# Attention scores of a hybrid encoder: two products over 128 rows, or three over 64 rows with two heads side by side

## The chip, the core and the metric

The kernel runs on one core of a Trainium2 chip. The engines of the core that matter here are TensorE (PE; its weight loads are shown as PEld), VectorE (DVE), ScalarE (ACT), GpSimd (POOL) and SyncE (SP), whose queue issues nearly all DMAs. The metric is device time in microseconds, lower is better: before the change the median of three runs was 1366.57 us (1365.75 to 1369.16).

## The reference

Two layers of an encoder over 512 tokens of width 1024, in fp32. Each layer adds to x a mixer of two head groups, a cross attention to 256 memory tokens, and a gated feed-forward block with a convolution of width 3. The change touches the scores of the mixer alone:

```python
def hybrid_mixer(h, w_in, rpb, q_norm, k_norm, w_out, rows, cos, sin):
    proj = h @ w_in
    na_q, na_k, na_v, g_q, g_k, g_v = jnp.split(proj, IN_SPLIT_POINTS, axis=-1)
    na_out = neighbourhood_attention(na_q, na_k, na_v, rpb, rows)      # 8 heads of 64
    g_q = apply_axial_rope(rms_norm(g_q, q_norm), cos, sin)            # 8 heads of 64
    g_k = apply_axial_rope(rms_norm(g_k, k_norm), cos, sin)            # 2 heads of 64
    gqa_out = gqa_block_attention(g_q, g_k, g_v)
    return jnp.concatenate([na_out, gqa_out], axis=-1) @ w_out

# neighbourhood_attention
scores = jnp.einsum('brqhd,brikhd->bhrqik', q, k_rows) * (dh ** -0.5)
# gqa_block_attention, one block of 128 queries
sc = jnp.einsum('bqkgd,bskd->bkgqs', qi, k) * scale
```

A score is a sum over the 64 elements of a head. The mixer's neighbourhood attention (NA) has, for a block of 128 queries, a window of 256 keys; its grouped-query attention (GQA) looks at all 512 keys.

## The kernel before

**Arithmetic.** TensorE is given operands in a reduced fp32 form (`F32R`). To keep fp32's accuracy, each operand is held as a rounded part and the difference to it, hi and lo, and a product of two operands is made as hi*hi + hi*lo + lo*hi, three matmuls into one PSUM bank (`mm3`, L374). Values live transposed: a projection's result has 128 output channels on the partitions ("rows") and the 512 tokens on the columns, so one tile holds two heads of 64, one on rows 0 to 63, the other on rows 64 to 127.

**Scores before.** A sum over 64 elements would use half of the rows, so the kernel fills the other half with the lo part. `split_q` (L735) writes for each head j a tile with q's hi on the head's own 64 rows and its lo on the other 64. `split_k` (L717) writes for each head k's hi twice, on both halves, and k's lo twice. Two matmuls over 128 rows then give (q_hi + q_lo) * k_hi and (q_hi + q_lo) * k_lo. A result must be written to both halves, which engines do in instructions of 64 rows: each head has its own ScalarE copy (the rounding) and its own VectorE difference. The doubling of k is done by two DMAs a tile (`double`, put into SP's queue), but for the first k tile of layer 0 (`near`), where ScalarE and VectorE write both halves themselves.

**Groups.** The mixer runs in units. `na_scores` (L778) makes 8 units a layer (4 head pairs, 2 pairs of query blocks), each with 2 heads, 2 blocks, 2 products: 8 matmuls of 256 columns. `gqa_scores` (L947) makes 16 units a layer (4 head pairs, 4 query blocks), each with 2 heads, 2 products: 4 matmuls of 512 columns. Behind the scores follow a row maximum on VectorE (L797, L959), the exponential on ScalarE (L803, L961), the division (L809, L967, L522), transposes on TensorE (`na_transpose`, `gqa_transpose_p`), and the products with the values (`na_values`, `gqa_values`).

**Order.** TensorE and SP run in program order. `weave` (L170) lines the steps of several units up, each unit's steps in different rounds, and puts matmuls of other work (projections of coming heads, output projection, memory keys) between them through a `Filler`. How much filler comes in goes by a count of TensorE time, `Counted.ns` (L67), which adds for a matmul of n columns max(107, (n+32)/2.4) ns; in the GQA part each round has a slot of counted time (`GQA_SLOT`, L49), and the filler fills up what the round's own steps leave. `late(n, fn)` puts a step off by n x 3600 counted ns (the doubling DMAs by 2, the steps of the rotary embedding by 1 or 2 each). Work on ScalarE, VectorE and GpSimd is ordered by a scheduler. Projection results are read from PSUM (`split_qk` L704; tags `mm`, 4 banks, `sc`, 2 banks, `tr`, 2 banks); a bank is given to the next product when its readers are done. SBUF tiles of the tag `r` come from a pool of 21.

For the GQA heads `gqa_rope` (L895) does norm and rotation in steps: products with gain and tables on VectorE (L901, L902), a square on ScalarE (L903), a swap of rows by DMA, a sum on GpSimd, a spread of the norm on TensorE, and then `split` (L933), which calls the same `split_q` and `split_k`.

The helper that the change uses in their place exists already, for values and for the memory attention:

```python
def split_psum(hi, lo, ps, scale=None):
    if scale is None:
        read(ACT.copy(hi, ps))
        DVE.tensor_sub(lo, ps, f(hi))
```

Of the kernel before, what the change touches and what calls it, by code (L numbers as in the profile page):

```python
# [18 lines left out]
P = 128  # L19
S = 512  # L20
# [25 lines left out]


NA_FILL = 2500
GQA_SLOT = [3950] * 16 + [4200, 3300, 3000, 3000]  # L49
MEM_FILL = [1, 1, 2, 2, 1, 3, 1, 3, 1, 3, 1]  # L50
N_ROWS = 3
LATE = 3600
# [14 lines left out]
class Counted(InOrder):  # L67


    ns = 0.0  # L70

    def matmul(self, out, lhsT, rhs, **k):
        n = 1
        for d in rhs.shape[1:]:
            n *= d
        self.ns += max(107.0, (n + 32) / 2.4)
        return self.tc.keep_in_program_order(self.engine.matmul(out, lhsT, rhs, **k))  # L77


# [104 lines left out]
def encoder_kernel(ctx: ExitStack, tc: tile.TileContext, t: dict, out: bass.AP):  # L184
    nc = tc.nc
    PE, SP = Counted(tc, nc.tensor), InOrder(tc, nc.sync)
    late = Late(PE)
    ACT_IN_ORDER = InOrder(tc, nc.scalar)
    ACT, DVE, POOL = Free(nc.scalar), Free(nc.vector), Free(nc.gpsimd)
# [24 lines left out]
    def rtile(shape, dt=F32R):  # L214
        return rpool.tile([P, *shape], dt, tag="r", name=nm("r"), padded_shape=[P, *pad(shape)])
# [7 lines left out]
    def rpair():  # L223

        hl = rtile((2, S))
        return hl[:, 0, :], hl[:, 1, :]
# [13 lines left out]
    f = lambda ap: ap.bitcast(F32)  # L240
# [10 lines left out]
    def read(e):  # L251
        reads.append(e.ins)
        return e
# [362 lines left out]
    for n in FIRST:  # L616
# [10 lines left out]
        k = slice(k0, k1)  # L627
# [15 lines left out]
    for l in range(DEPTH):  # L643
# [60 lines left out]
        def split_qk(n, p, pm):  # L704
            if n == "q":
                DVE.scalar_tensor_tensor(pm, pm, HD**-0.5, mix.rep, op0=ALU.mult, op1=ALU.mult)
                st = rtile((2, S))
                qk[n, p] = [st[:, j] for j in range(2)]
                split_q(pm, st)
                return  # L710
            DVE.tensor_mul(pm, pm, mix.rep)

            kt = [rtile((2, S)) for _ in range(2)]
            qk[n, p] = [kt[j][:, part] for part in range(2) for j in range(2)]
            split_k(pm, kt, (l, p) == (0, 0))

        def split_k(pm, kt, near):  # L717
            rows = [(slice(64 * j, 64 * j + 64), slice(64 - 64 * j, 128 - 64 * j)) for j in range(2)]
            for k, (r, o) in zip(kt, rows):
                read(ACT.copy(k[r, 0], pm[r]))  # L720
                if near:
                    ACT.copy(k[o, 0], pm[r])
            for k, (r, o) in zip(kt, rows):
                DVE.tensor_sub(k[r, 1], pm[r], f(k[r, 0]))
                if near:
                    DVE.tensor_sub(k[o, 1], pm[r], f(k[r, 0]))

            def double():
                for k, (r, o) in zip(kt, rows):
                    SP.dma_start(f(k[o]), f(k[r]))  # L730

            if not near:
                late(2, double)

        def split_q(pm, st):  # L735
            halves = [(st[:, j], slice(64 * j, 64 * j + 64), slice(64 - 64 * j, 128 - 64 * j)) for j in range(2)]
            for v, r, o in halves:
                read(ACT.copy(v[r], pm[r]))  # L738
            for v, r, o in halves:
                DVE.tensor_sub(v[o], pm[r], f(v[r]))  # L740

        vblk = [None, None]

# [34 lines left out]
        def na_scores(u):  # L778
            p, bp = divmod(u, 2)
            if bp == 0 and p + 1 < 4:  # L780
                load_bias(p + 1)
            qst, kst = qk["q", p], qk["k", p]
            sc = [ps_s().rearrange("p (i n) -> p i n", i=2) for _ in range(2)]
            for i in range(2):
                b = 2 * bp + i
                qs, ks = slice(b * P, b * P + P), slice(WIN[b], WIN[b] + 256)
                for j in range(2):
                    for part in range(2):
                        PE.matmul(sc[j][:, i, :], qst[j][:, qs], kst[2 * part + j][:, ks], start=part == 0, stop=part == 1)
            nmx, sums = small(4), small(4)  # L790
            es = [tmp((2, 256)) for _ in range(2)]
            with behind(30):
                for j in range(2):
                    for i in range(2):
                        b = 2 * bp + i
                        col = slice(2 * j + i, 2 * j + i + 1)
                        DVE.tensor_tensor_reduce(  # L797
                            out=sc[j][:, i, :], in0=sc[j][:, i, :], in1=bias[p][j][:, WTYPE[b], :],
                            op0=ALU.add, op1=ALU.min, scale=-1.0, scalar=BIG, accum_out=nmx[:, col])
                for j in range(2):  # L800
                    for i in range(2):
                        col = slice(2 * j + i, 2 * j + i + 1)
                        ACT.activation(es[j][:, i, :], sc[j][:, i, :], AF.Exp, bias=nmx[:, col], scale=-1.0,  # L803
                                       accum_out=sums[:, col])
            na[u] = es, sums
# [89 lines left out]
        def gqa_rope(g, pm):  # L895


            gain = qkg[:, l, 0:1] if g != "k" else qkg[:, l, 1:2]
            xs, sq, cc = tmp(), tmp(), tmp()
            with behind(-20):  # L900
                DVE.scalar_tensor_tensor(xs, pm, gain, gtab[0][:, 1], op0=ALU.mult, op1=ALU.mult)  # L901
                DVE.scalar_tensor_tensor(cc, pm, gain, gtab[0][:, 0], op0=ALU.mult, op1=ALU.mult)  # L902
                read(ACT.activation(sq, pm, AF.Square))  # L903

            def swap():
                xr = tmp()
                for i in range(4):
                    SP.dma_start(xr[32 * i : 32 * i + 32], xs[32 * (i ^ 1) : 32 * (i ^ 1) + 32])
                pv = ps_t()
                for b in range(NB):  # L910
                    PE.matmul(pv[:, 2 * b : 2 * b + 2], sq[:, b * P : (b + 1) * P], pairs, start=True, stop=True)
                v, r = small(2 * NB), small(2 * NB)
                DVE.scalar_tensor_tensor(
                    v.rearrange("p (b j) -> p b j", j=2), pv[:, 0 : 2 * NB].rearrange("p (b j) -> p b j", j=2),
                    1.0 / HD if g == "k" else 1.0, geps[:, int(g != "k")].unsqueeze(2).to_broadcast([P, NB, 2]),
                    op0=ALU.mult, op1=ALU.add)
                rows = tmp()
                with behind(-40):
                    POOL.tensor_tensor(r, v, mhalf[:, : 2 * NB], op=ALU.pow)
                    POOL.tensor_copy(rows.rearrange("p (b d) -> p b d", d=HD), r.unsqueeze(2).to_broadcast([P, 2 * NB, HD]))  # L920
                late(1, lambda: rotate(xr, rows))

            def rotate(xr, rows):
                POOL.tensor_add(xr, cc, xr)
                late(2, lambda: norm(xr, rows))

            def norm(xr, rows):
                pr = ps_mm()
                for b in range(NB):
                    PE.matmul(pr[:, b * P : (b + 1) * P], rows[:, b * P : (b + 1) * P], ident, start=True, stop=True)  # L930
                late(1, lambda: split(xr, pr))

            def split(xr, pr):  # L933
                DVE.tensor_mul(pr, xr, pr)
                if g == "k":
                    gk.extend(rtile((2, S)) for _ in range(2))
                    split_k(pr, gk, False)
                else:
                    gq[g] = rtile((2, S))
                    split_q(pr, gq[g])  # L940

            late(1, swap)

# [3 lines left out]
        def gqa_scores(u):  # L947
            i, b = divmod(u, NB)
            qs = slice(b * P, b * P + P)
            assert gq[i] is not None and gk and gvt  # L950
            sc = [ps_s() for _ in range(2)]
            for j in range(2):
                for part in range(2):
                    PE.matmul(sc[j], gq[i][:, j, qs], gk[j][:, part], start=part == 0, stop=part == 1)
            nmx, sums = small(2), small(2)
            es = []
            for j in range(2):
                c = slice(j, j + 1)
                DVE.tensor_reduce(nmx[:, c], sc[j], axis=AX.X, op=ALU.max, negate=True)  # L959
                e = tmp()  # L960
                last_exp[0] = read(ACT.activation(e, sc[j], AF.Exp, bias=nmx[:, c], accum_out=sums[:, c])).ins  # L961
                es.append(e)
            ga[u] = es, sums
# [25 lines left out]
        def gqa_values(u, j):  # L989
# [2 lines left out]
            i, bp = divmod(u // 2, 2)  # L992
            if j == 0:
                gpo[u] = ps_mm().rearrange("p (j n) -> p j n", j=2)
            po, pts = gpo[u], gpt[u // 2]
            for k in range(NB):
                for n in range(2):
# [459 lines left out]
```

## Time and profile before

| | us |
|---|---|
| median of three runs | 1366.57 |
| profiled execution | 1367.86 |
| its span, first to last instruction | 1366.1 |
| TensorE busy in the span | 1349.0 |
| VectorE busy | 877.3 |
| ScalarE busy | 675.0 |
| GpSimd busy | 688.1 |

How to read it: in the rows of a timeline stand the start and the length in us, the engine, the line, the operation, the tiles (out<-in, with a short name for a pool's tiles), the shape and the number of instructions merged into the row; in brackets the idle time ahead of it and what ended it. The line of a matmul is that of a helper (L77 for all in-order matmuls, L64 for transposes), so products are told apart by their tiles: `sc<-r,r` are scores, `tr<-ident,t` transposes. In the groups stand the shape, the count, busy time and mean length in ns, and the idle time just before. Matmuls overlap: the length of a record is longer than the distance from one start to the next. In the rows of a window stand its limits, its length, and busy time and count of each engine (PE, PEld, DVE, ACT, POOL), then the granted TensorE clock, the DMA share and GB/s.

### The profile page before, as it was taken

How to read it: one execution, taken by the hardware profiler on the slowest of the kernel's cores; microseconds unless marked ns; L12 is line 12 of the kernel's file. 1: busy time of each engine (PE TensorE's matmuls, PEld its weight loads, DVE VectorE, ACT ScalarE, POOL GpSimd, SP SyncE). 2: the span in 40 equal slices, each digit the busy share in tenths (PEclk: the TensorE clock that was granted, in tenths of full speed). 3: DMA queues.
4: the chain of work that ended last, by engine and by line, in shares of the span. 5: the costliest groups of instructions: out<-in, count | busy, mean ns of one | idle time of the engine just before them, and what ended most of it. 6: DMA issues, size and time to landing. Idle time of an engine off the chain costs nothing.

```text
span 1366.1 us, 19239 instructions
## 1 busy us (share of the span) xinstructions
PE 1349.0 (99%) x7082; PEld 1157.5 (85%) x7082; DVE 877.3 (64%) x1542; ACT 675.0 (49%) x1258; POOL 688.1 (50%) x491
## 2 busy tenths in 40 slices
PE   9999999999999999999999999999999999999998
PEld 7888899888888888888888988998888888888897
DVE  6665776665886188357546777746758834861874
ACT  6675577564543144234456667756644423432441
POOL 2466657636444444444554676657264444444441
PEclk9999999999999999999999999999999999999999
DMA  6753213322333333333347532133143333323331
GB/s 215 212 169 99 77 47 86 86 77 77 104 98 93 95 98 92 102 94 98 87 121 227 140 101 70 57 100 94 31 123 93 101 100 93 101 84 109 93 92 63
DMA packets 219358, 139.88 MB, mean 102 GB/s; under 512 B 6144, under 2 KB 212224, under 8 KB 219264
## 3 DMA queue, kind: packets, MB, share of 16 engines
q1 hardware_dynamic: 218432, 138.13, 34.5%
q8 instruction: 56, 0.92, 0.3%
q10 hardware_dynamic: 832, 0.53, 0.1%
q14 instruction: 38, 0.31, 0.1%
HBM read 126.05 MB, written 2.10 MB: 94 GB/s over the span
## 4 chain that ended last, share of the span: by engine, by line
PE 91%; DVE 3%; ACT 3%; DMA 2%; issue 1%; SPq 0%; POOL 0%; DVEq 0%; ACTq 0%
PE mm L77 80%; PE sc L77 6%; PE tr L64 3%; PE tr L77 1%; DMA raw<-in_w_in 1%; DMA t<-in_memT 1%; ACT t L803 1%; ACT hi L290 0%; SPq L64 0%; DMA xT<-in_xT 0%; DVE t L487 0%; ACT r L515 0%; DVE sc L797 0%; DVE r L740 0%; ACT r L738 0%
## 5 line engine op out<-in xcount | busy, mean ns | idle before, releaser
L291 POOL TENSOR_TENSOR lo<-raw,hi 128x1024 fp32r<-128x1024 f32 (+2 forms) x268 | 499.9, 1876 | 477.1 <-ACT hi L290 472.7
L77 PE MATMUL mm<-xg,hi 128*128 128x512 f32 x1920 | 596.6, 392 | 0.0
L77 PEld LDWEIGHTS mm<-xg,hi 128*128 128x128 f32 x1920 | 356.7, 188 | 70.8
L290 ACT CAST hi<-raw 128x512 fp32r<-128x512 f32 (+2 forms) x276 | 224.1, 836 | 309.5 <-PE mm L77 256.3
L77 PE MATMUL mm<-xg,lo 128*128 128x512 f32 x960 | 374.5, 390 | 0.0
L77 PE MATMUL mm<-r,hi 128*128 128x512 f32 (+1 forms) x1096 | 316.6, 373 | 0.0
L77 PEld LDWEIGHTS mm<-r,hi 128*128 128x128 f32 x1096 | 198.3, 189 | 34.7 <-DVE r L516 0.4
L1281 DVE SCALAR_TENSOR_TENSOR t<-t,par,t 128x7 f32<-128x7 f32 (+1 forms) x352 | 201.8, 641 | 34.0 <-ACT t L1274 34.0
L77 PEld LDWEIGHTS mm<-xg,lo 128*128 128x128 f32 x960 | 180.7, 188 | 38.2
L77 PE MATMUL mm<-r,lo 128*128 128x512 f32 (+1 forms) x548 | 203.5, 371 | 0.0
L77 PEld LDWEIGHTS mm<-r,lo 128*128 128x128 f32 x548 | 103.3, 188 | 17.8
L1266 DVE TENSOR_TENSOR t<-mm,rep 128x512 f32<-128x512 f32 x88 | 60.1, 687 | 78.6 <-PE mm L77 62.3
L522 POOL TENSOR_SCALAR t<-t,s 128x512 f32<-128x512 f32 (+1 forms) x112 | 66.8, 610 | 78.0 <-DVE s L809 36.8
L1287 DVE TENSOR_TENSOR r<-t,r 128x512 fp32r<-128x512 f32 x44 | 90.2, 2049 | 7.3 <-ACT r L1286 4.1
L1283 ACT ACTIVATE t<-t 128x512 f32<-128x512 f32 x44 | 27.9, 633 | 134.4 <-DVE t L1281 134.3
L1310 DVE TENSOR_TENSOR xT<-xT,mm 128x512 f32<-128x512 f32 x32 | 21.9, 685 | 106.8 <-PE mm L77 106.8
L77 PE MATMUL sc<-r,r 128*128 128x256 f32 (+1 forms) x352 | 70.0, 332 | 0.0
L1274 ACT ACTIVATE t<-t,par 128x512 f32<-128x512 f32 x88 | 66.8, 806 | 3.3 <-DVE t L1266 3.3
L64 PE MATMUL tr<-ident,t 128*128 128x128 f32 x456 | 62.0, 276 | 2.3 <-DVE t L522 0.9
L77 PE MATMUL mm<-r,r 128*128 128x256 f32 (+1 forms) x428 | 61.9, 297 | 2.4 <-ACT t L903 2.4
L64 PEld LDWEIGHTS tr<-ident,t 128*128 128x128 f32 x456 | 53.3, 142 | 10.5 <-issue 2.9
L77 PEld LDWEIGHTS mm<-r,r 128*128 128x128 f32 x428 | 56.3, 191 | 5.1 <-ACT t L903 2.6
(156 smaller groups left out, 1618.2 us busy)
## 6 DMA issues: line engine op xcount, KB each, us to landing
raw<-in_w_up SPq DMA_DIRECT2D x88, 512.0 KB, 3.7
raw<-in_w_in SPq DMA_DIRECT2D x33, 512.0 KB, 3.9
raw<-in_w_down SPq DMA_DIRECT2D x32, 448.0 KB, 3.6
raw<-in_w_mem_kv SPq DMA_DIRECT2D x16, 512.0 KB, 3.6
raw<-in_w_down SPq DMA_DIRECT2D x16, 512.0 KB, 3.9
r<-in_bias SPq DMA_DIRECT2D x16, 384.0 KB, 5.6
r<-r SPq DMA_DIRECT2D x22, 256.0 KB, 5.0
raw<-in_w_out SPq DMA_DIRECT2D x8, 512.0 KB, 3.6
```

What stands on the lines that cost most here:

```text
L64: return lambda *a, **k: self.tc.keep_in_program_order(op(*a, **k))
L77: return self.tc.keep_in_program_order(self.engine.matmul(out, lhsT, rhs, **k))
L290: act.copy(hi[:, k], raw[:, k])
L291: (POOL if eng[0] == "P" else DVE).tensor_sub(lo[:, k], raw[:, k], f(hi)[:, k])
L522: eng.tensor_scalar(e, e, sums[:, col : col + 1], 1.0, op0=ALU.mult, op1=ALU.mult)
L803: ACT.activation(es[j][:, i, :], sc[j][:, i, :], AF.Exp, bias=nmx[:, col], scale=-1.0, accum_out=sums[:, col])
L1266: DVE.tensor_mul(u, us[side], ffn.rep)
L1274: ACT.activation(cc, u, AF.Identity, bias=par[:, l, CB + ch : CB + ch + 1], scale=w[1])
L1281: DVE.scalar_tensor_tensor(cc[:, dst], u[:, src], wi, cc[:, dst], op0=ALU.mult, op1=ALU.add)
L1283: ACT.activation(cs[0], cs[0], AF.Silu)
L1287: DVE.tensor_sub(acts[j][1], cs[0], f(acts[j][0]))
L1310: DVE.tensor_add(xT[m], xT[m], pm)
```

## The change

q and k are held as the projection leaves them, both heads in one tile, one tile for hi and lo: a single copy and a single difference over 128 rows. The halves are not doubled, so the DMAs and the `near` case go. A score is now three products over the 64 rows of its head, q_hi*k_hi + q_hi*k_lo + q_lo*k_hi; the two heads' products alternate, one on rows 0 to 63, the other on rows 64 to 127, each into its own bank. An NA unit has 12 matmuls in place of 8, a GQA unit 6 in place of 4. The count takes a matmul of 64 rows at half, and 150 ns for each change of the number of rows; 16 slots grow by 100 ns. The check that the value tile exists moves from the scores to the values. (lo*lo, which the two products of before included, is left out, as in `mm3`.)

```diff
-GQA_SLOT = [3950] * 16 + [4200, 3300, 3000, 3000]
+GQA_SLOT = [4050] * 16 + [4200, 3300, 3000, 3000]
...
-    ns = 0.0
+    ns, rows = 0.0, P
 
     def matmul(self, out, lhsT, rhs, **k):
...
-        self.ns += max(107.0, (n + 32) / 2.4)
+        rows = lhsT.shape[0]
+        if rows != self.rows:
+            self.ns += 150.0
+        self.rows = rows
+        self.ns += max(107.0, (n + 32) / 2.4) * rows / P
...
         def split_qk(n, p, pm):
             if n == "q":
                 DVE.scalar_tensor_tensor(pm, pm, HD**-0.5, mix.rep, op0=ALU.mult, op1=ALU.mult)
-                st = rtile((2, S))
-                qk[n, p] = [st[:, j] for j in range(2)]
-                split_q(pm, st)
-                return
-            DVE.tensor_mul(pm, pm, mix.rep)
-
-            kt = [rtile((2, S)) for _ in range(2)]
-            qk[n, p] = [kt[j][:, part] for part in range(2) for j in range(2)]
-            split_k(pm, kt, (l, p) == (0, 0))
-
-        def split_k(pm, kt, near):
...
-        def split_q(pm, st):
...
+            else:
+                DVE.tensor_mul(pm, pm, mix.rep)
+
+            qk[n, p] = rpair()
+            split_psum(*qk[n, p], pm)
+
+        def pair_scores(sc, q, k, qs, ks):
+
+            (qh, ql), (kh, kl) = q, k
+            for n, (a, b) in enumerate(((qh, kh), (qh, kl), (ql, kh))):
+                for j in range(2):
+                    r = slice(64 * j, 64 * j + 64)
+                    PE.matmul(sc[j], a[r, qs], b[r, ks], start=n == 0, stop=n == 2)
...
-                for j in range(2):
-                    for part in range(2):
-                        PE.matmul(sc[j][:, i, :], qst[j][:, qs], kst[2 * part + j][:, ks], start=part == 0, stop=part == 1)
+                pair_scores([v[:, i, :] for v in sc], qk["q", p], qk["k", p], qs, ks)
...
                 if g == "k":
-                    gk.extend(rtile((2, S)) for _ in range(2))
-                    split_k(pr, gk, False)
+                    gk.extend(rpair())
+                    split_psum(*gk, pr)
                 else:
-                    gq[g] = rtile((2, S))
-                    split_q(pr, gq[g])
+                    gq[g] = rpair()
+                    split_psum(*gq[g], pr)
...
-            assert gq[i] is not None and gk and gvt
+            assert gq[i] is not None and gk
             sc = [ps_s() for _ in range(2)]
-            for j in range(2):
-                for part in range(2):
-                    PE.matmul(sc[j], gq[i][:, j, qs], gk[j][:, part], start=part == 0, stop=part == 1)
+            pair_scores(sc, gq[i], gk, qs, slice(0, S))
...
+            assert gvt
             po, pts = gpo[u], gpt[u // 2]
```

More of the change, by code (lines that the diff above doesn't have):

```diff
@@ L706, in split_qk @@
                 DVE.scalar_tensor_tensor(pm, pm, HD**-0.5, mix.rep, op0=ALU.mult, op1=ALU.mult)
-                st = rtile((2, S))
-                qk[n, p] = [st[:, j] for j in range(2)]
-                split_q(pm, st)
-                return
-            DVE.tensor_mul(pm, pm, mix.rep)
-            kt = [rtile((2, S)) for _ in range(2)]
-            qk[n, p] = [kt[j][:, part] for part in range(2) for j in range(2)]
-            split_k(pm, kt, (l, p) == (0, 0))
-        def split_k(pm, kt, near):
[L718 to L733, printed above, removed]
-        def split_q(pm, st):
[L736 to L740, printed above, removed]
+            else:
[8 more added lines that the diff above has]
+                    PE.matmul(sc[j], a[r, qs], b[r, ks], start=n == 0, stop=n == 2)
         vblk = [None, None]
@@ L781, in na_scores @@
                 load_bias(p + 1)
-            qst, kst = qk["q", p], qk["k", p]
             sc = [ps_s().rearrange("p (i n) -> p i n", i=2) for _ in range(2)]
```

## The prediction

> **What bounds the kernel now.** I read the page first (busy shares, then the chain that ended last), then the groups by line and shape, then TensorE's own timeline around the scores, then its waits.
>
> ```profile
> span 1366.1 us, 19239 instructions
> PE 1349.0 (99%) x7082; PEld 1157.5 (85%) x7082; DVE 877.3 (64%) x1542; ACT 675.0 (49%) x1258; POOL 688.1 (50%) x491
> PE 91%; DVE 3%; ACT 3%; DMA 2%; issue 1%; SPq 0%; POOL 0%; DVEq 0%; ACTq 0%
> PE mm L77 80%; PE sc L77 6%; PE tr L64 3%; PE tr L77 1%; DMA raw<-in_w_in 1%; DMA t<-in_memT 1%; ACT t L803 1%; ACT hi L290 0%; SPq L64 0%; DMA xT<-in_xT 0%; DVE t L487 0%; ACT r L515 0%; DVE sc L797 0%; DVE r L740 0%; ACT r L738 0%
> ```
>
> TensorE is the bound: 99% busy, 91% of the chain. VectorE and ScalarE have room (64%, 49%), so work taken from them is worth something only where TensorE waits for it. What the change does to the time is therefore, first, what it does to the length of TensorE's stream inside the score groups, and second, what it does to the few waits.
>
> ```profile
> L77 PE MATMUL mm<-r,lo 128*128 128x512 f32 x456 | 177.5, 389 | 0.0
> L77 PE MATMUL sc<-r,r 128*128 128x512 f32 x128 | 37.1, 412 | 0.0
> L77 PE MATMUL sc<-r,r 128*128 128x256 f32 x224 | 32.9, 287 | 0.0
> ```
>
> The 128 score matmuls of 512 columns are the GQA ones: 2 layers x 16 units x 2 heads x 2 products, so 32 groups of 4. Of the 224 with 256 columns, 96 are the memory attention's (2 x 8 x 2 x 3, untouched); 128 are the neighbourhood attention's (NA): 2 x 8 units x 2 blocks x 2 heads x 2 products, 16 groups of 8. The mean of a record is not what one costs, since records overlap; the distance of starts is.
>
> ```profile
> 40.24 1.12 PE L77 MATMUL sc<-r,r 128*128 128x256 f32 x8
> 41.20 0.28 PE L77 MATMUL mm<-hi,xg 128*128 128x256 f32 x1
> ...
> 148.24 1.07 PE L77 MATMUL sc<-r,r 128*128 128x512 f32 x4
> 149.15 0.61 PE L77 MATMUL mm<-r,hi 128*128 128x512 f32 x2
> ...
> 179.96 1.03 PE L64 MATMUL tr<-ident,t 128*128 128x128 f32 x8
> 180.75 1.17 PE L77 MATMUL sc<-r,r 128*128 128x512 f32 x4
> 181.75 1.11 PE L77 MATMUL mm<-xg,r 128*128 128x256 f32 x8
> ```
>
> An NA group takes 41.20 - 40.24 = 0.96 us, 0.12 for a matmul of 256 columns. A GQA group takes 0.91 us behind another full matmul (0.227 each) and 1.00 behind transposes, the usual place: the mean record of 412 against 389 is 23 ns on each of 4, so nearly all 32 groups carry these 0.09 us. All score matmuls of this kind together are 16 x 0.96 + 32 x 1.00 = 47 us. That is the whole field on which the products can win or lose.
>
> **The change, part by part.**
>
> *The products.* Each group goes from two products a head over 128 rows to three over 64 rows, the two heads alternating between the lower and the upper half: NA 12 matmuls instead of 8, GQA 6 instead of 4. If the halves work side by side, matmul time is three pairs: NA 6 x 0.12 = 0.72, GQA 3 x 0.227 = 0.68. But every matmul brings its own weight load, 384 instead of 256 in all, and the trace shows a floor for those:
>
> ```profile
> 151.94 0.95 PE L77 MATMUL tr<-pairs,t 128*128 128x2 f32 x8
> 152.75 0.71 PE L77 MATMUL mm<-r,hi 128*128 128x512 f32 x2
> 153.30 0.39 PE L77 MATMUL mm<-r,lo 128*128 128x512 f32 x1
> ```
>
> Eight matmuls of two columns take 0.81 us, 0.101 each, where the columns are next to nothing: that is one load after another. A load of 64 rows has the same 128 columns, so I price it the same, 0.10. NA then needs 12 x 0.101 = 1.21 us, bound by loads, above the 0.96 of now; GQA's 6 x 0.101 = 0.61 stay under its 0.68. If instead the loads of the two halves run together, NA is 0.72: these are the two ends. I take 1.21, since every row of this trace that is short of columns sits on that floor.
>
> *The switches.* Each of the 48 groups now lies between full-height work: 48 changes of height in, 48 out. No row of before has one. The lower end is nothing beyond what is paid now. For the upper end the array would have to empty, then load with nothing to hide it. Emptying is at most the record beyond its distance, 389 - 227 = 0.16 us. An unhidden load is seen where TensorE restarts after a wait:
>
> ```profile
> 38.70 0.39 PE L77 MATMUL mm<-hi,xg 128*128 128x256 f32 x1 [1.41 <-DVE r L740]
> 38.93 0.28 PE L77 MATMUL mm<-lo,xg 128*128 128x256 f32 x1
> 39.05 0.40 PE L77 MATMUL mm<-hi,xg 128*128 128x256 f32 x2
> ```
>
> The second start comes 0.23 after the first instead of 0.12, so 0.11 for the load; in the rows above, from transposes to full matmuls, 0.55 - 0.45 = 0.10 is much the same. So a switch lies between 0 and 0.27 us. I take 0.16: more than a restart alone, as an array in work has to be emptied first, and less than both, as part of the load should pass during the emptying. In a GQA group the switch in takes the place of the 0.09 paid behind transposes.
>
> The Trainium skill, "TensorEngine Tiling (Array Packing)", Key Properties, speaks against the change here: changing the tiling mode, not just the tile, drains TensorE. No row of before can show it; taken in full, it makes the 0.27 of the upper end (the second rival).
>
> *Sum on TensorE.* NA: 1.21 + 2 x 0.16 - 0.96 = +0.57, x 16 = +9.1 us. GQA: 0.68 + 2 x 0.16 - 1.00 = 0.00, x 32 = 0.
>
> *The evictions.* Splits of q and k now take one copy and one difference of full height instead of two of half height.
>
> ```profile
> L740 DVE TENSOR_TENSOR r<-mm,r 64x512 fp32r<-64x512 f32 x28 | 19.3, 689 | 10.0 <-ACT r L738 9.7
> L724 DVE TENSOR_TENSOR r<-mm,r 64x512 fp32r<-64x512 f32 x16 | 11.0, 688 | 5.1 <-ACT r L720 4.8
> L738 ACT CAST r<-mm 64x512 fp32r<-64x512 f32 x28 | 16.3, 580 | 8.9 <-DVE mm L934 5.6 <-DVE mm L706 3.1
> L516 DVE TENSOR_TENSOR r<-mm,r 128x512 fp32r<-128x512 f32 x16 | 10.9, 688 | 12.7 <-ACT r L515 12.7
> L515 ACT CAST r<-mm 128x512 fp32r<-128x512 f32 x16 | 9.4, 586 | 9.6 <-PE mm L77 9.6
> ```
>
> Half the rows cost the same: 64x512 takes 689 ns, 128x512 takes 688. The half-height differences are 32 for 16 splits of q, 20 for 10 of k and 2 more for the near one:
>
> ```profile
> L740 DVE TENSOR_TENSOR r<-sc,r 64x512 fp32r<-64x512 f32 x4 | 2.8, 689 | 0.7 <-ACT r L738 0.6
> L724 DVE TENSOR_TENSOR r<-sc,r 64x512 fp32r<-64x512 f32 x4 | 2.8, 689 | 0.8 <-ACT r L722 0.7
> L726 DVE TENSOR_TENSOR r<-sc,r 64x512 fp32r<-64x512 f32 x2 | 1.4, 688 | 0.0
> ...
> 32.31 1.39 DVE L740 TENSOR_TENSOR r<-sc,r 64x512 fp32r<-64x512 f32 x2
> 37.26 1.39 DVE L740 TENSOR_TENSOR r<-mm,r 64x512 fp32r<-64x512 f32 x2
> ```
>
> With the 28 and 16 above that is 54, and as many copies; 26 of each remain. VectorE is freed of 28 x 0.69 = 19 us and ScalarE of 28 x 0.58 = 16 us. Almost all of it lies under TensorE's stream and is worth nothing. It counts at the start of layer 0: between 32.31 and 38.65 eight half-height differences run (q0 two, k0 four, q1 two), and the wait at 38.70 above, 1.41 us, is TensorE waiting for the last. Three would end 5 x 0.69 = 3.4 us earlier, so I take this wait as gone: -1.4 us. If something else is late there, it is 0.
>
> *The copies by DMA.*
>
> ```profile
> r<-r SPq DMA_DIRECT2D x22, 256.0 KB, 5.0
> ```
>
> Of these 22 the straddling value blocks keep 4; the 18 that double k go, and with them their places in SP's queue. TensorE's waits name none of them, so that is 0; their going takes no cover from anything. k is ready earlier, and nothing waits for it now.
>
> *The bookkeeping.* The counted time of a GQA group goes from 907 ns (4 x 544/2.4) to 680 + 2 x 150 = 980, +73, and a slot grows by 100: 27 ns more filler in each of 16 slots, 0.4 us a layer that is pulled forward from the rest, whose total is fixed. The later check on the value tile lets scores be emitted before it, no instruction more. Both change order only: 0, with one exception among the rivals.
>
> **Total**: +9.1 + 0 - 1.4 = +7.7 us against the profiled execution, 1367.86 us (span 1366.1 and 1.8 around it) = 1375.6. The runs' median, 1366.57, lies 1.3 lower, so 1374.
>
> **The rivals.**
>
> *Cheap switches and paired loads (faster).* If the two halves load together, NA is 0.72; with switches at 0 to 0.08, NA changes by -0.24 to -0.08 (x 16 = -3.8 to -1.3) and GQA by -0.23 to -0.16 (x 32 = -7.3 to -5.1; at 0 the 0.09 stays). With -1.4 that is -12.5 to -7.8: 1354 to 1359. It decides for faster from NA groups under 0.96. For it: loads already pass under matmuls all over the trace. Against: the floor of 0.101 is kept everywhere. The Trainium skill, "TensorE: Matmul & The Clock Gate", What overlaps and what doesn't, has loads overlapping matmuls in flight when their row groups differ, which is this rival; no run here shows it yet.
>
> *Full emptying and bare loads.* Switches at 0.27: NA +0.79 x 16 = 12.6, GQA +0.22 x 32 = 7.0, -1.4: +18.3, 1385. For it: restarts do show the bare load. Against: it has to come on top of the emptying each time.
>
> *The halves don't work side by side.* Then the change doesn't do what it says: NA 12 x 0.12 = 1.44, GQA 6 x 0.227 = 1.36. With no price on switches +7.7 + 14.4 - 1.4 = +20.7, 1387; with 0.16, +33, 1400. Against: nothing in the trace, which has no matmul of half height.
>
> *The stall at 118 us goes.* TensorE's longest wait:
>
> ```profile
> PE mm L77 <- ACT t L903: 2.4, 1, 2.4
> ...
> 117.94 0.18 DVE L809 RECIPROCAL s<-s 128x4 f32<-128x4 f32 x1 [1.60 <-ACT t L803]
> 118.22 0.70 DVE L934 TENSOR_TENSOR mm<-t,mm 128x512 f32<-128x512 f32 x1
> ...
> 122.00:130.00 8.00, 8.00 (x31) 6.98 (x30) 2.74 (x7) 3.11 (x7) 5.92 (x5) 0.57 0.48 147
> ```
>
> VectorE stood 1.60 us behind a reciprocal, and what frees TensorE's bank queued after it. The stall is followed by a granted clock of 0.57 over 8 us, another 3.4 us. A new order could remove both: -5.8, so 1368.5; a similar stall elsewhere costs as much, 1380. For it: the order of VectorE's work in layer 0 is dealt anew. Against: the reciprocal waits for exponentials, not for splits, and the change leaves these alone.
>
> **How the numbers follow.** Forecast 0.38, own range 1367 to 1378 (switches of 0.08 to 0.20: +0.1 to +11.6). Cheap switches 0.25; full emptying 0.15; not side by side 0.10; the stall gone 0.12. Runs of this kernel tell about 0.3%, 4.1 us, from no change: same is 1362.5 to 1370.7. Slower: most of the forecast (0.27), 0.15, 0.10 and a third of the last (0.04) = 0.56. Faster: 0.25, and 0.03 of the others = 0.28. Same: 0.16. The range 1355 to 1391 holds the forecast, the emptying, the stall either way, nearly all of the cheap case and the lower end of not side by side.
>
> **What would show it.** Score matmuls of 64 rows whose pairs start close together, groups of 6 over 0.7 us (side by side) or 1.4 (not). NA groups of 12 at 1.2 us for loads one by one, 0.7 for paired loads. The distance from the last full-height start before a group, and from the last of the group to the next, less the normal distance, is the switch. The wait at 38.7 for the q split should be missing, and so should 28 copies and 28 differences. The prediction is wrong if NA groups take 0.96 us or less with their switches, or if a wait of TensorE longer than 2 us stands in a place where before had none.

## The result, and the profile after

The changed kernel takes 1370.15 us (median of 7 runs, 1368.37 to 1372.03), the kernel before 1366.06 beside it (7 runs): a ratio of 1.003, 95% interval [1.0018, 1.0041]. That is 4.1 us slower, where 7.7 were forecast.

The page of the profiled execution after (its time 1369.62 us):

```profile
span 1367.8 us, 19361 instructions
PE 1352.3 (99%) x7210; PEld 1142.5 (84%) x7210; DVE 858.7 (63%) x1514; ACT 656.4 (48%) x1230; POOL 688.7 (50%) x491
PE 92%; ACT 2%; DMA 2%; DVE 1%; issue 1%; POOL 1%; SPq 0%; DVEq 0%; ACTq 0%; POOLq 0%
```

TensorE has 128 instructions more (384 score matmuls for 256). VectorE is busy for 18.6 us less, and ScalarE also for 18.6; the 28 differences and 28 copies that went make 19 and 16 us by the prediction's rows. The time didn't follow them: TensorE is still 99% busy and 92% of the chain.

The groups of the scores by shape:

```profile
L82 PE MATMUL sc<-r,r 64*128 64x512 f32 x192 | 30.9, 427 | 0.0
L82 PE MATMUL sc<-r,r 64*128 64x256 f32 x192 | 15.6, 294 | 0.0
```

The mean record of one matmul is about as long as before (427 ns against 412, 294 against 287, where the 287 is a mean with the memory attention's), but 192 matmuls of 512 columns are busy for less time than 128 were: 30.9 us against 37.1. They lie on top of each other. TensorE's timeline shows it, first around an NA group, then around a GQA group:

```profile
37.52 0.28 PE L82 MATMUL mm<-lo,xg 128*128 128x256 f32 x1
37.64 0.28 PE L82 MATMUL mm<-hi,xg 128*128 128x256 f32 x1
37.85 0.98 PE L82 MATMUL sc<-r,r 64*128 64x256 f32 x12
38.75 0.39 PE L82 MATMUL mm<-hi,xg 128*128 128x256 f32 x1
38.98 0.28 PE L82 MATMUL mm<-lo,xg 128*128 128x256 f32 x1
...
177.60 1.03 PE L64 MATMUL tr<-ident,t 128*128 128x128 f32 x8
178.57 0.96 PE L82 MATMUL sc<-r,r 64*128 64x512 f32 x6
179.47 1.22 PE L82 MATMUL mm<-xg,r 128*128 128x256 f32 x8
180.53 0.63 PE L82 MATMUL mm<-r,hi 128*128 128x512 f32 x2
```

Twelve matmuls in 0.90 us (37.85 to 38.75) can't be one after another at 0.12: they run as six pairs. In the single records the two of a pair start 3 to 4 ns apart; the second pair comes 0.22 us behind the first, the others 0.12 apart, and the next full matmul starts 0.21 behind the last pair. So there is time at both edges that the matmuls' own distance doesn't need. Into the group, the start comes 0.21 after the last full matmul, 0.09 more than its 0.12. Out of it, 38.75 to 38.98 is 0.23, 0.11 more. From the last full start before the group to the second after it an NA group now takes 37.64 to 38.98 = 1.34 us; before it was 0.12 + 0.96 + 0.12 = 1.20. So +0.14.

For GQA, take the stretch from the start of the transposes to the end of the value matmuls behind the scores: 177.60 to 180.53 = 2.93 us. Before, its rows are

```profile
179.96 1.03 PE L64 MATMUL tr<-ident,t 128*128 128x128 f32 x8
180.75 1.17 PE L77 MATMUL sc<-r,r 128*128 128x512 f32 x4
181.75 1.11 PE L77 MATMUL mm<-xg,r 128*128 128x256 f32 x8
182.70 0.63 PE L77 MATMUL mm<-r,hi 128*128 128x512 f32 x2
```

and 182.70 - 179.96 = 2.74. So +0.19 by these rows, which are the upper end. From the single records of both traces, from the last start before a group to the second behind it, in groups with the same neighbours before and after: NA +0.144 in the mean of 13 groups (0.137 to 0.157), GQA +0.172 in the mean of 29 (0.155 to 0.193). Over all groups that is 16 x 0.144 + 32 x 0.172 = 2.3 + 5.5 = 7.8 us more in TensorE's stream.

TensorE's waits give part of it back. After, some of the list:

```profile
PE mm L82 <- DVE r L521: 1.3, 1, 1.3
...
PE mm L82 <- DVE t L832: 1.1, 1, 1.1
```

The wait for the q split at 38.7 us (1.4) is gone, as forecast, and in place of the 2.4 us at 118 us there is one of 1.1 (L832). A new one of 1.3 us stands at 61.93:

```profile
59.20 2.07 DVE L296 TENSOR_TENSOR lo<-raw,hi 128x512 fp32r<-128x512 f32 x2
61.20 0.68 DVE L521 TENSOR_TENSOR r<-tr,r 128x512 fp32r<-128x512 f32 x1
61.93 0.39 PE L82 MATMUL mm<-r,r 128*128 128x256 f32 x1 [1.28 <-DVE r L521]
```

Here VectorE works off two differences of weights (2.07 us) before the one on whose result the value matmuls wait. The waits listed for TensorE sum to 10.6 us before and 8.2 after, 2.4 less. 7.8 - 2.4 = 5.4 us; the medians are 4.1 apart. Single executions of one program differ in their waits and in their clock by about as much as what lies between (below).

### The profile page after: what moved, and what is told of

It reads as the page before. It is cut to its first block, busy times and chain, and to the rows that moved or that the text cites. A ratio compares the mean times of both kernels' runs of the same rounds, so it can differ in the third digit from the quotient of the medians.

```text
span 1367.8 us, 19361 instructions
## 1 busy us (share of the span) xinstructions
PE 1352.3 (99%) x7210; PEld 1142.5 (84%) x7210; DVE 858.7 (63%) x1514; ACT 656.4 (48%) x1230; POOL 688.7 (50%) x491
## 4 chain that ended last, share of the span: by engine, by line
PE 92%; ACT 2%; DMA 2%; DVE 1%; issue 1%; POOL 1%; SPq 0%; DVEq 0%; ACTq 0%; POOLq 0%
PE mm L82 82%; PE sc L82 6%; PE tr L64 4%; PE tr L82 1%; DMA raw<-in_w_in 1%; POOL lo L296 1%; ACT hi L295 0%; DMA xT<-in_xT 0%; ACT t L784 0%; DMA t<-in_memT 0%; ACT r L520 0%; ACT t L64 0%; SPq L64 0%; DVE sc L778 0%; DVE r L573 0%
## 5 line engine op out<-in xcount | busy, mean ns | idle before, releaser
L82 PE MATMUL sc<-r,r 64*128 64x256 f32 (+2 forms) x480 | 61.5, 347 | 0.0
```

## The experiments

The theory from the two traces, called the switch theory: the halves do work side by side, and what is lost is the change of height, 96 times about 0.2 us. Against it: the halves only partly overlap, the weight loads come one by one as predicted, or the loss is in the order of the work. "Over the kernel after" is against its 1370.15; the ratios are against the kernel before, run beside each version.

**Full rows: no switches, nothing side by side.**

```diff
-                    r = slice(64 * j, 64 * j + 64)
+                    r = slice(0, P)
```

> The kernel after, but each of the three products takes all 128 rows instead of its head's 64: a head's scores then hold the other head's sum too (the split by head is left out). Order of work and evictions as after; no change of height anywhere. Switch theory (the halves work side by side, each change of height costs about 0.2 us): NA groups go to 12 x 0.12 = 1.44 us, GQA groups to 6 x 0.227 = 1.36; from starts around the groups that is +0.34 us x 16 and +0.28 x 32, so about 14 us over the kernel after, 1384. If the halves did not work side by side, the groups would not get longer and the 96 switches would be saved: 1350 or less.

The other lines of the edit, here and in the next run, keep the counted time, and with it the filler, as in the kernel after (and give the scores a line of their own, L726).

Measured: 1381.8 us (ratio 1.012 [1.0103, 1.0137]), 11.7 over the kernel after. Its NA group stands in the stream without a gap at either edge:

```profile
38.94 0.28 PE L82 MATMUL mm<-hi,xg 128*128 128x256 f32 x1
39.06 1.60 PE L726 MATMUL sc<-r,r 128*128 128x256 f32 x12
40.50 0.28 PE L82 MATMUL mm<-hi,xg 128*128 128x256 f32 x1
40.62 0.28 PE L82 MATMUL mm<-lo,xg 128*128 128x256 f32 x1
```

0.12 in, 1.44 for twelve, 0.12 out.

**One half: switches, nothing side by side.**

```diff
-                    r = slice(64 * j, 64 * j + 64)
+                    r = slice(0, 64)
```

> The kernel after, but both heads' products take rows 0 to 63 (head 1 repeats head 0's scores, its own are left out). Switches stay, side by side goes. Switch theory: matmul time as with full rows, 1.44 and 1.36 us a group, plus two switches each: +0.72 x 16 + 0.68 x 32 = 33 us over the kernel after, 1403, and the distance to the run with full rows, 19 us over 96 switches, is 0.2 us for each. If only rows, not halves, mattered: no longer than after, 1370.

Measured: 1399.72 us (ratio 1.0252 [1.0234, 1.0269]), 29.6 over the kernel after.

```profile
38.71 0.28 PE L82 MATMUL mm<-hi,xg 128*128 128x256 f32 x1
38.92 1.69 PE L726 MATMUL sc<-r,r 64*128 64x256 f32 x12
40.54 0.38 PE L82 MATMUL mm<-hi,xg 128*128 128x256 f32 x1
40.76 0.28 PE L82 MATMUL mm<-lo,xg 128*128 128x256 f32 x1
```

The same twelve matmuls of 64 rows take 1.62 us on one half and 0.90 on two: side by side is worth 29.6 us in this kernel. The edges are those of the kernel after, 0.21 and 0.22. The two runs differ by 17.9 us in 96 switches: 0.19 us each, the 0.09 and 0.11 seen at the edges made into a price by a whole kernel. Both runs came out 2 to 3 us under what was expected; TensorE's waits sum to 5.3 and 4.3 us in them, against 8.2 in the kernel after, which makes up for it. The 1400 that the prediction gave for halves that don't work side by side is what this run takes.

**Two groups: more switches, not one matmul more.** The third pair is issued behind the value matmuls of head 0.

```diff
-            pair_scores(sc, gq[i], gk, qs, slice(0, S))
+            pair_scores(sc, gq[i], gk, qs, slice(0, S), (0, 1))
+            ga[u] = sc
+
+        def gqa_scores_end(u):
...
+            pair_scores(sc, gq[i], gk, qs, slice(0, S), (2,))
...
-        weave(4 * NB, [..., (0, gqa_scores), (3, lambda u: gqa_values(u, 0)),
+        weave(4 * NB, [..., (0, gqa_scores), (3, lambda u: gqa_values(u, 0)), (0, gqa_scores_end),
```

> The kernel after, with each GQA group cut: its first two pairs, then the value matmuls of head 0 that used to follow the scores, then the third pair. In every second unit there are such value matmuls, so 16 groups become two: 32 switches more, not one instruction more. Switch theory: 32 x 0.2 = +6 us over the kernel after, 1376. If the loss lies in waits and in the order of the work instead: within 2 us of the kernel after.

Measured: 1374.37 us (ratio 1.0062 [1.0046, 1.0078]), 4.2 over the kernel after. In its timeline a group that stays whole and one that is cut follow each other:

```profile
177.77 1.04 PE L64 MATMUL tr<-ident,t 128*128 128x128 f32 x8
178.73 0.97 PE L82 MATMUL sc<-r,r 64*128 64x512 f32 x6
179.63 1.22 PE L82 MATMUL mm<-xg,r 128*128 128x256 f32 x8
180.69 0.63 PE L82 MATMUL mm<-r,hi 128*128 128x512 f32 x2
...
182.76 1.03 PE L64 MATMUL tr<-ident,t 128*128 128x128 f32 x8
183.73 0.73 PE L82 MATMUL sc<-r,r 64*128 64x512 f32 x4
184.39 1.22 PE L82 MATMUL mm<-xg,r 128*128 128x256 f32 x8
185.54 0.50 PE L82 MATMUL sc<-r,r 64*128 64x512 f32 x2
185.96 0.73 PE L82 MATMUL mm<-r,hi 128*128 128x512 f32 x2
186.53 0.40 PE L82 MATMUL mm<-r,lo 128*128 128x512 f32 x1
```

Whole: 2.92 us to the next filler. Cut: 3.20, and the filler's first two matmuls need 0.57 instead of 0.46: +0.39 for two switches. The expectation counted 16 groups; only 12 were cut, as the first rounds of each layer have no values yet. 24 x 0.19 = 4.6 fits the 4.2, and nothing but the order of the same matmuls was changed. The loss isn't in waits: they sum to 6.4 us here, less than the 8.2 of the kernel after.

**The slot.** `GQA_SLOT` back to 3950 in the kernel after.

> The kernel after with slots of 3950 counted ns as before. Filler is only dealt out later, its total is fixed: within 2 us of the kernel after by the switch theory. If the slot were what costs: back to 1366.

Measured: 1369.66 us (ratio 1.0029 [1.0018, 1.004]), within 0.5 us of the kernel after. The slot costs nothing that these runs can tell. The trace shows something more. Up to 160 us the instructions of the four engines come in the same order as in the kernel after, yet the 1.3 us at 61.9 are missing, and all waits sum to 6.7 us. On the other hand the clock is at 0.51 from 786.90 to 790.40 us, 1.7 us lost, where the execution of the kernel after shows 1.00. Such pieces come and go between executions.

**NA alone, GQA alone.** Each part of the mixer gets the change without the other; in the first the slots are those of before.

> Only the NA scores and their q and k splits are changed, GQA stays with two products over 128 rows (slots of 3950). Switch theory: 16 groups at 0.90 us plus two switches against 0.96, +0.14 us each from the starts around them, +2.2 us, and the first wait at 38.7 us gone, -1.4: within 2 us of before, 1367. By the predicted sum (loads one by one) it should carry the whole loss: +9.1 - 1.4, 1374.

> Only the GQA scores and their splits are changed (slots of 4050), NA stays with two products over 128 rows. Switch theory: +0.175 us x 32 groups = +5.6 us: 1372. By the predicted sum: 0, 1366.

Measured: NA alone 1365.96 us (ratio 1.0001 [0.9993, 1.0009]); GQA alone 1370.44 (1.0037 [1.0024, 1.005]), against 1365.79 of before. NA is a tie, within about 1.2 us by its interval: its +2.3 us in the stream and the waits it removes are about even (they sum to 8.3 us, against 10.6 before). GQA alone is 4.7 us over before, the whole loss as far as these runs can tell; its clocks are a little lower (0.994 to 0.998), so part of that can be clock. The predicted split, +9.1 for NA and 0 for GQA, is refuted in both halves.

**Early pairs.** The kernel before, with the pairs and the full-height splits for the first two head pairs of layer 0 only.

> The kernel before, with the pairs and the full-height splits only for the first two head pairs of NA in layer 0, where TensorE waited 1.41 us for the split. Switch theory: 4 groups x 0.14 = +0.55, the wait gone -1.4: 1365, a candidate for the best. If the wait only moves: 1366 to 1367.

Measured: 1366.46 us (ratio 1.0003 [0.9992, 1.0013]): no gain that can be told. The wait at 38.7 is gone, but others have come, 12.1 us in all against 10.6. One is at the place where the profiled execution of the kernel after has its wait:

```profile
60.45 0.74 PE L84 MATMUL mm<-r,r 128*128 128x256 f32 x4 [0.34 <-DVE r L523]
62.97 0.74 PE L84 MATMUL mm<-r,r 128*128 128x256 f32 x4 [1.77 <-DVE r L523]
```

**Before again.** The kernel before, for its clock.

> The kernel before, unchanged, for the clock of its executions. If the stretch of half clock behind the 2.4 us stall at 118 us belongs to this kernel, nearly every execution shows a granted clock of about 0.996 against 0.998 and more after, and the kernel after has gained about 3 us there; if it is chance, the clocks spread as widely as after's.

Measured: 1365.8 us (12 runs), and a granted clock of 0.998 in the profiled execution, as after. The stall at 118 us is there as ever, but the window behind it differs from that of the first execution, which had 0.57:

```profile
118.00:122.00 4.00, 1.63 (x9) 1.40 (x9) 2.54 (x5) 2.29 (x6) 3.48 (x6) 0.97 0.20 49
122.00:130.00 8.00, 8.00 (x38) 6.76 (x38) 3.86 (x8) 3.79 (x8) 6.34 (x6) 0.80 0.45 139
```

In the kernel after, the same window has the full clock:

```profile
122.00:130.00 8.00, 8.00 (x49) 7.00 (x48) 6.50 (x11) 3.90 (x9) 6.63 (x5) 1.00 0.38 123
```

The lost clock is 0.43 x 8 = 3.4 us in the first, 0.20 x 8 + 0.03 x 4 = 1.7 in the second. Behind the same stall of 2.4 us in the run with GQA alone the clock stays at 1.00 from 122 to 130 us. It varies from execution to execution, and only 7 of 42 executions of the kernel before have a mean clock of 0.996 or less (all 42: 0.995 to 0.999; the kernel after, 7 executions: 0.997 to 0.999), so the expectation that it belongs to the kernel fell. Without it the three spans are 1366.1 - 3.4 = 1362.7 and 1364.1 - 1.7 = 1362.4 before, 1367.8 after: 5.1 to 5.4 us apart, as counted from groups and waits (5.4).

None of these versions beats the kernel before.

## Why the prediction was right, point by point

The sign held, and the size in part: 1374 was forecast, 1370.15 measured, within the range 1367 to 1378; +7.7 became +4.1. By the prediction's own band (1362.5 to 1370.7) that is still "same", to which it gave 0.16 against 0.56 for slower, though the interval of the ratio, from 1.0018, leaves out no change. And the terms inside were wrong in opposite directions: NA +9.1 for +2.3, GQA 0 for +5.5, waits -1.4 for -2.4. That their sum came near is luck.

- *The halves work side by side*: right. One half costs 29.6 us over two, so the rival in which they don't is out; and the pairs keep the 0.12 us of one full matmul, so the overlap isn't a partial one either.
- *Weight loads one by one, 12 x 0.101 = 1.21 us for an NA group*: wrong. In a layer 1 group the twelve loads lie in 0.77 us (their merged row): loads of the two halves pass together, and the group of 0.91 is six pairs at 0.12, 0.10 of a bare load and 0.09 before the next matmul. The price of one load was off too: in 0.81 for eight matmuls of two columns the first starts 0.03 in front of the second, behind a long matmul, and the others are 0.11 apart, as transposes are (below). The Trainium skill, "TensorE: Matmul & The Clock Gate", What overlaps and what doesn't, has loads overlap matmuls in flight only when their row groups differ. The loads of the two halves pass with each other's matmuls here, as by that rule, but the trace doesn't bear out the "only": a full-height load starts at 707.49 while full-height matmuls run, from 707.36 to 707.76.

```profile
707.36 0.40 PE L82 MATMUL mm<-hi,xg 128*128 128x256 f32 x2
707.49 0.19 PEld L82 LDWEIGHTS mm<-lo,xg 128*128 128x128 f32 x1
707.60 0.28 PE L82 MATMUL mm<-lo,xg 128*128 128x256 f32 x1
...
707.93 0.77 PEld L82 LDWEIGHTS sc<-r,r 64*128 64x128 f32 x12
707.93 0.98 PE L82 MATMUL sc<-r,r 64*128 64x256 f32 x12
708.84 0.19 PEld L82 LDWEIGHTS mm<-hi,xg 128*128 128x128 f32 x1
708.84 0.39 PE L82 MATMUL mm<-hi,xg 128*128 128x256 f32 x1
```

- *A switch at 0.16 us, between 0 and 0.27*: close, 0.19. Both parts are in the records: 0.09 from the last matmul of one height to the first of the other, beyond the normal distance, and 0.10 to 0.11 for the first load, which nothing hides. That load starts with its matmul (707.93 and 708.84, both rows) instead of one matmul ahead (707.49 for 707.60). Emptying, if that is what the first part is, adds only 0.09, not the 0.16 of record length over distance; so the second rival (0.27, +18 us) stayed out. The Trainium skill, "TensorEngine Tiling (Array Packing)", Key Properties, says that changing the tiling mode drains TensorE. The trace agrees in that every change of height costs time, 0.19 us with the load.
- *In GQA the switch in replaces the 0.09 paid behind transposes*: wrong, and this is the step that hid GQA's loss. From the timeline of before: eight transposes; the last two of them again, in a view that starts there; and the group behind:

```profile
175.13 1.03 PE L64 MATMUL tr<-ident,t 128*128 128x128 f32 x8
175.79 0.38 PE L64 MATMUL tr<-ident,t 128*128 128x128 f32 x2
175.93 1.17 PE L77 MATMUL sc<-r,r 128*128 128x512 f32 x4
```

Six transposes take 175.79 - 175.13 = 0.66, 0.11 each, so two would take 0.22; but the long matmul starts 0.14 after the first of the last two, 0.08 early. Of the 0.09 to 0.10 by which the group is longer, 0.08 is that early start; what is paid is 0.02. So a group cost about 0.93, and 0.68 + 0.38 is 0.13 more, not 0. The 0.17 measured is a little over that: in a GQA group the two switches take 0.41.
- *NA*: with paired loads and 0.19, 0.72 + 0.38 - 0.96 = +0.14, as measured, not +0.57.
- *The evictions*: 28 copies and 28 differences went, worth nothing but at one wait, as argued. The wait at 38.7 did go. In the profiled execution 1.3 of its 1.4 us came back at 61.9, where VectorE is late for another reason, and the early pairs show a wait there too; but in the run with the old slots, the same up to that point, there is none. So what the -1.4 is worth to the time stays open; all waits together fell by 2.4.
- *DMAs and slot at 0*: right for the slot by its own run; for the DMAs no run was made, but TensorE waits for none of them.
- *The stall at 118 us*: halved (2.4 to 1.1). That its half clock would return 3.4 us was read from one execution; another lost 1.7.
- *Its own signs of being wrong*: neither came. An NA group takes 0.72 + 0.38 = 1.10 us with its switches, over the 0.96, and no wait is longer than 1.3 us.

## What to carry to other kernels

Two half-height products side by side save half of their matmul time, but a group of them pays two changes of height, 0.38 to 0.41 us here, in a stream that is otherwise full height. So count the groups, not the matmuls: 0.24 us saved in an NA group against 0.38 paid loses, and so does 0.23 against 0.41 in a GQA group. An estimate from these numbers: a group would have to be 1.6 to 1.8 times as long to come out even; no run here has such a group. When a group's cost is read from a timeline, measure between starts of the same kind on both sides, so that an overlap at its edge isn't booked as a cost.

## What the runs showed of the hardware that was not expected

Weight loads into the two halves pass together: a pair of 64-row matmuls with a load each keeps the 0.12 us of one matmul of 256 columns, while full-height matmuls with fewer columns stay 0.11 apart (transposes). And the half clock behind a stall isn't fixed: behind the same 2.4 us, 3.4 us were lost in one execution of the kernel before, 1.7 in another and none with GQA alone. The run with the old slots lost 1.7 at 787 us behind a wait of 0.9, and the kernel after, which has this wait too, nothing there.
